# Attention layer: the last group's units in another order, and the last output tile's right half held in PSUM

## The chip, the cores and the metric

The kernel runs on one core of one Trainium2 chip. The metric is the device time of one execution in microseconds. TensorE (PE in the rows; its weight loads are PEld), VectorE (DVE), ScalarE (ACT) and GpSimd (POOL) each work through a queue of their own in order; SyncE (SP) issues most of the DMAs. Engines wait for one another by semaphores.

## The reference, cut to what matters

One layer: an RMS norm, an attention mixer with three branches, an output projection, a second RMS norm and the residual. S = 512 tokens, D = 1024, 16 heads of 64 in 4 groups of 4 heads (a group shares its keys and values).

```python
def rms_norm(x, gain):
    y = xf * lax.rsqrt(jnp.mean(xf * xf, axis=-1, keepdims=True) + RMS_EPS)
    return (y * gain.astype(jnp.float32)).astype(x.dtype)

def nsa_mixer(h, w_in, w_out, ...):
    q, kv, g, z = split_cols(h @ w_in, ...)
    gates, zs = jax.nn.sigmoid(g), jax.nn.silu(z)
    o_cmp, p_cmp = nsa_compressed(q, kc, vc, table)     # 31 compressed keys
    o_slc = nsa_selected(q, k_s, v_s, sel, table)       # with 8 blocks, all that are causal
    o_win = nsa_window(q, k_w, v_w, table)              # window of 512
    y = jnp.sum(gates * stack([o_cmp, o_slc, o_win]) * zs, axis=2)
    return y @ w_out                                     # (512 x 1024) @ (1024 x 1024)

h = x + rms_norm(nsa_mixer(rms_norm(x, pre_gain), ...), post_gain)
```

## The kernel before

Every float32 factor of a matmul is split into a high and a low part, and a product is three matmuls (high by high, high by low, low by high). `split_raw` makes the parts of a weight tile of 128x1024: a cast on ACT (L106, 1.05 us) and a subtraction on POOL (L109, 2.4 us); the raw tiles come by DMA into three buffers `wr`, the parts lie in three buffers each, `wh` and `wl`.

The attention goes over four groups g. A group has seven units: `win` for query tiles 3, 2, 1, then `both` (window and selected branch of query tile 0, and the compressed branch of all tiles), then `slc` for query tiles 1, 2, 3. A unit of query tile qt has qt + 1 key tiles. `qk(u)` makes its scores head by head (matmuls L582 into a bank `s`), DVE adds the bias and takes the extreme (L594), ACT exponentiates (L595). `pv(u)` transposes the probabilities (L676 into a bank `t`), ACT casts the high part `pth` (L679), DVE subtracts for the low part `ptl` (L680), and L684 and L685 multiply with the values into the one bank `o`. ACT copies the halves that are crossed (L690, L691), DVE adds them (L692, L693), POOL multiplies with the gate `zf` and adds into the group's `y` (L697, L698). In the last group `split_y(3, qt)` then casts the tile's y to a high part on ACT (L764), subtracts on DVE (L765), and puts qt on the list `ready`. `cmp_pv` is the compressed branch: two rounds of L747 to L749 in bank `o`, a product (L751) and an addition into y (L752) on DVE.

The program is written by hand in this order: `qk` of unit i is woven with `pv` of unit i - 1, and between their steps a generator `fill` is pulled for projections, at a rate per group; what is left of it at the end runs alone. The last piece of `fill` is `wout`, the output projection. For the halves c of the output columns it first accumulates the three finished groups (kp = 0, 1, 2; matmuls L804 to L806) in two banks `pj`, two tiles of rows at a time, and ACT copies the sums to `og` (L809). Then, for each tile t in the order of `ready` (0, 1, 2, 3), it adds the last group: per half six matmuls (L845 to L847) in a bank `pj`, an addition into `og` on DVE (L849), ACT's Square with its sum (L851); then the sum of both halves on POOL (L855), `rstd` on POOL (L85, L86), the gain multiplies (L853, L858 on POOL, L859 on DVE or POOL), and, one tile later, `finish`: `og * rstd + x` on DVE (L828) and the store (L829). PSUM has eight banks: two `pj`, three `s`, two `t`, one `o`.

The framework that builds the program gives each engine its instructions in an order of its own choosing near the written one; what that order is stands in the section on the change.

## Time and profile before

| | before |
|---|---|
| three timed runs | 486.06 us median, 485.45 to 486.08 |
| profiled execution | 485.76 us, of which the span of its instructions is 484.0 us |
| PE busy | 456.1 us (94%), mean granted clock 0.986 |
| DVE busy | 329.9 us (68%) |
| ACT busy | 274.2 us (57%) |
| POOL busy | 184.3 us (38%) |

The span goes from the first to the last instruction. Busy shares are means over stages with different limits. Matmuls are pipelined and their ends are modelled, so that one of 512 columns shows 0.39 us and the next starts 0.23 us after it.

### The profile page before, as it was taken

The page shows a single profiled execution, that of the slowest core. Times are in us where ns is not written, and L with a number is a line of the kernel's source. Part 1 is how long each engine was busy: PE and PEld are TensorE (multiplying, and loading weights), DVE is VectorE, ACT ScalarE, POOL GpSimd, SP SyncE. Part 2 cuts the span into 40 slices and gives each one's busy share as a digit, 9 for nine tenths or more (in the row PEclk, how much of TensorE's full clock was granted, in tenths as well). Part 3 has the DMA queues.
Part 4 walks back from the last instruction along what each step waited for, and adds up shares of the span by engine and source line. Part 5 has one row for each costly group of instructions (what it writes and reads, how often), then busy time and mean ns, then how long its engine had stood idle before and what let it go on. Part 6 is the DMA issues. An engine that isn't in the chain of part 4 may idle for free.

```text
span 484.0 us, 6882 instructions
## 1 busy us (share of the span) xinstructions
PE 456.1 (94%) x2330; PEld 375.2 (78%) x2330; DVE 329.9 (68%) x785; ACT 274.2 (57%) x644; POOL 184.3 (38%) x147
## 2 busy tenths in 40 slices
PE   5999999999999989999999999998899999999982
PEld 3898788878888768878888788886678888777761
DVE  6779752745456897665788874679867465876576
ACT  5613232436556858556587764576766456755541
POOL 3414543424124345333154343342514314342556
PEclk9989999999999999999999999999999999999996
DMA  8498455443023122321130511322152112031123
GB/s 289 140 90 256 141 165 173 126 137 80 16 82 86 41 70 65 112 85 45 43 110 1 175 44 45 87 53 58 45 173 86 46 45 87 1 89 43 57 75 130
DMA packets 45501, 44.63 MB, mean 92 GB/s; under 512 B 7751, under 2 KB 38471, under 8 KB 45466
## 3 DMA queue, kind: packets, MB, share of 16 engines
q1 hardware_dynamic: 44424, 44.00, 32.4%
q8 instruction: 18, 0.29, 0.3%
q10 hardware_dynamic: 1042, 0.20, 0.2%
q14 instruction: 17, 0.14, 0.1%
HBM read 41.99 MB, written 2.20 MB: 91 GB/s over the span
## 4 chain that ended last, share of the span: by engine, by line
PE 74%; ACT 9%; DVE 8%; POOL 4%; issue 3%; DMA 1%; POOLq 0%; SPq 0%; DVEq 0%; ACTq 0%
PE ps_pj L139 9%; PE ps_pj L137 9%; PE ps_pj L138 9%; PE ps_s L582 7%; PE ps_t L676 6%; PE ps_o L685 3%; ACT p L595 3%; PE ps_o L684 3%; PE ps_s L238 2%; PE ps_s L240 2%; PE ps_s L239 2%; PE ps_pj L239 2%; PE ps_pj L238 2%; PE ps_pj L240 2%; PE ps_s L667 1%
## 5 line engine op out<-in xcount | busy, mean ns | idle before, releaser
L109 POOL TENSOR_TENSOR wl<-wr,wh 128x1024 fp32r<-128x1024 f32 x49 | 118.5, 2419 | 163.7 <-ACT wh L106 150.2
L137 PE MATMUL ps_pj<-uh,wh 128*128 128x512 f32 x240 | 99.4, 414 | 0.0
L138 PE MATMUL ps_pj<-uh,wl 128*128 128x512 f32 x240 | 94.4, 393 | 0.0
L139 PE MATMUL ps_pj<-ul,wh 128*128 128x512 f32 x240 | 94.3, 393 | 0.0
L595 ACT ACTIVATE p<-p,nm 128x512 f32<-128x512 f32 (+3 forms) x128 | 71.6, 561 | 37.5 <-DVE nm L594 36.8
L106 ACT CAST wh<-wr 128x1024 fp32r<-128x1024 f32 x49 | 51.3, 1048 | 42.5 <-DMA wr<-in_nsa_w_in_dram 14.8
L680 DVE TENSOR_TENSOR ptl<-ps_t,pth 128x512 fp32r<-128x512 f32 x80 | 54.7, 686 | 21.0 <-ACT pth L679 20.5
L582 PE MATMUL ps_s<-kd,q 128*128 128x512 f32 (+5 forms) x256 | 61.7, 328 | 0.0
L679 ACT CAST pth<-ps_t 128x512 fp32r<-128x512 f32 x80 | 46.0, 579 | 23.1 <-PE ps_t L676 22.3
L139 PEld LDWEIGHTS ps_pj<-ul,wh 128*128 128x128 f32 x240 | 45.1, 188 | 9.9
L582 PEld LDWEIGHTS ps_s<-kd,q 128*128 128x128 f32 x256 | 45.4, 188 | 9.2 <-DVE nm L594 0.2
L594 DVE CUSTOM_DVE_ANT_0 p<-ps_s,bias 128x128 f32<-128x128 f32 (+3 forms) x80 | 34.7, 447 | 23.1 <-PE ps_s L582 22.6
L138 PEld LDWEIGHTS ps_pj<-uh,wl 128*128 128x128 f32 x240 | 45.3, 189 | 5.8
L137 PEld LDWEIGHTS ps_pj<-uh,wh 128*128 128x128 f32 x240 | 45.2, 188 | 5.3
L676 PE MATMUL ps_t<-ident,p 128*128 128x128 f32 x320 | 48.9, 272 | 0.0
L676 PEld LDWEIGHTS ps_t<-ident,p 128*128 128x128 f32 x320 | 39.3, 140 | 6.7
L684 PE MATMUL ps_o<-pth,vt 128*128 128x512 f32 x80 | 32.8, 411 | 2.5 <-DVE otmp L693 1.1
L685 PE MATMUL ps_o<-ptl,vt 128*128 128x512 f32 x80 | 32.5, 406 | 1.0 <-DVE ptl L680 1.0
L697 POOL TENSOR_TENSOR otmp<-otmp,zs 128x256 f32<-128x256 f32 x16 | 12.0, 748 | 48.4 <-DVE otmp L693 48.4
L695 POOL TENSOR_TENSOR y<-otmp,zs 128x256 f32<-128x256 f32 x16 | 11.8, 738 | 48.1 <-DVE otmp L693 48.1
L692 DVE TENSOR_TENSOR otmp<-ps_o,otmp 64x256 f32<-64x256 f32 x32 | 13.3, 415 | 21.8 <-ACT otmp L691 21.2
L594 DVE CUSTOM_DVE_ANT_1 p<-ps_s,bias 128x256 f32<-128x256 f32 (+2 forms) x48 | 25.9, 549 | 2.4 <-PE ps_s L582 2.1
(248 smaller groups left out, 899.8 us busy)
## 6 DMA issues: line engine op xcount, KB each, us to landing
wr<-in_nsa_w_in_dram SPq DMA_DIRECT2D x36, 512.0 KB, 3.7
wr<-in_nsa_w_in_dram SPq DMA_DIRECT2D x16, 256.0 KB, 4.3
bias<-toepd SPq DMA_DIRECT2D x16, 256.0 KB, 6.8
wr<-in_nsa_w_out_dram SPq DMA_DIRECT2D x8, 512.0 KB, 4.3
xt<-in_x_dram SPq DMA_DIRECT2D x4, 512.0 KB, 4.2
wr<-in_nsa_cmp_k_w_dram SPq DMA_DIRECT2D x4, 512.0 KB, 5.3
wr<-in_nsa_cmp_v_w_dram SPq DMA_DIRECT2D x4, 512.0 KB, 3.7
xr<-in_x_dram SPq DMA_DIRECT2D x8, 256.0 KB, 2.8
```

What stands on the lines that cost most here:

```text
L106: A.copy(h[:, 0:kn], raw[:, 0:kn])
L109: el.tensor_tensor(l[:, 0:kn], raw[:, 0:kn], h[:, 0:kn].bitcast(F32), op=ALU.subtract)
L137: T.matmul(p, a, rh, start=k == 0, stop=False)
L138: T.matmul(p, b, rh, start=False, stop=False)
L139: T.matmul(p, a, rl, start=False, stop=k == KT - 1)
L582: T.matmul(po, qs[h][:, qt * 128:(qt + 1) * 128], kds[h // R][:, i, c0:c0 + n], start=i == 0, stop=i == 1)
L594: V.tensor_tensor_reduce(pd, src, bi, 1.0, BIG, ALU.add, ALU.min, st["nm"][:, hh:hh + 1])
L595: A.activation(po, po, AF.Exp, bias=st["nm"][:, hh:hh + 1], scale=-1.0, accum_out=st["rs"][:, hh:hh + 1])
L676: T.transpose(tp[:, hh * 128:(hh + 1) * 128], st["p"][hh][:, c:c + 128], ident)
L680: V.tensor_tensor(pl, tp, ph.bitcast(F32), op=ALU.subtract)
L684: T.matmul(acc, v, prev[1], start=j == 1, stop=False)
L685: T.matmul(acc, v, prev[2], start=False, stop=j == qt + 1)
```

## The change

In the last group the three `slc` units run in the order 3, 2, 1, and `wout` takes its tiles in the order 0, 3, 2, 1 (`turn`); the compressed branch's gate is projected ahead of the selected one's in that group. The right half (c = 1) of the last tile is left out of the early accumulation. Its three finished groups are accumulated ahead of the third tile's last-group matmuls (18 matmuls, moved) into a bank `late`, the last group's six matmuls go into the same bank, and Square and the gain multiply read that bank, with no copy to `og` and no addition. The last group's weights `w3` get buffers of their own, those of earlier tiles. For the last two tiles the last group's sums use the banks `s`. The mean's 1/1024 goes into the Square as a scale of 1/32, and `rstd` adds both halves' sums and EPS in one instruction (L88 after; the power is L90). For the last unit the gate product and the addition into y, and for the last two tiles three gain multiplies, go from POOL to DVE. Line numbers after the change are higher: L582 is L589, L594 and L595 are L601 and L602, L667 is L674, L676 to L693 are L683 to L700, L695, L697 and L698 are L703, L705 and L706, L742 is L750, L764 and L765 are L772 and L773, L106 is L113, L804 to L806 stay and serve the last group too, L809 is L819, L828 is L841, L849 is L862, L851 is L864, L858 is L870, L859 is L871 (L866 for the last tile).

```diff
-    def rstd(dst, ss):
-        tc.keep_in_program_order(P.tensor_scalar(dst, ss, 1.0 / D, EPS, op0=ALU.mult, op1=ALU.add))
+    def rstd(dst, ss, other=None):
+        if other is None:
+            i = P.tensor_scalar(dst, ss, EPS, None, op0=ALU.add)
+        else:
+            i = P.tensor_scalar(dst, ss, other, EPS, op0=ALU.add, op1=ALU.add)
+        tc.keep_in_program_order(i)
         tc.keep_in_program_order(P.tensor_tensor(dst, dst, nhalf, op=ALU.pow))
...
-             (("win", 3), ("win", 2), ("win", 1), ("both", 0), ("slc", 1), ("slc", 2), ("slc", 3))]
+             [("win", 3), ("win", 2), ("win", 1), ("both", 0)] + [("slc", (t, 4 - t)[g == 3]) for t in (1, 2, 3)]]
...
+            eng = V if u == units[-1] else P
             if br == B_WIN:
-                P.tensor_tensor(y[:, :, qsl], tmp, zf, op=ALU.mult)
+                eng.tensor_tensor(y[:, :, qsl], tmp, zf, op=ALU.mult)
             else:
-                P.tensor_tensor(tmp, tmp, zf, op=ALU.mult)
-                P.tensor_tensor(y[:, :, qsl], y[:, :, qsl], tmp, op=ALU.add)
+                eng.tensor_tensor(tmp, tmp, zf, op=ALU.mult)
+                eng.tensor_tensor(y[:, :, qsl], y[:, :, qsl], tmp, op=ALU.add)
...
     def wout():
+        turn = [0, 3, 2, 1]
         og = [keep.tile([128, D], F32, name="og", tag="u", bufs=8) for _ in range(NT)]
         sumsq = const.tile([128, NT, 2], F32, name="sumsq")
 
-        def wo_tile(kp, c):
+        def wo_tile(kp, c, home=None):
             raw = load_raw([((lambda raw: raw.rearrange("p (k a) c -> p k (a c)", k=2)),
                              w_out[kp * 256:(kp + 1) * 256, c * S:(c + 1) * S].rearrange("(k p) c -> p k c", p=128))])
-            return [v.rearrange("p (k a) c -> p k (a c)", k=2) for v in split_raw(raw, 4, A, P)]
+            return [v.rearrange("p (k a) c -> p k (a c)", k=2) for v in split_raw(raw, 4, A, P, home)]
+
+        def wo_mm(p, kp, t, a, b, first, last):
+            ts = slice(t * 128, (t + 1) * 128)
+            for kk in range(2):
+                yh, yl = yhl[kp][0][:, kk, ts], yhl[kp][1][:, kk, ts]
+                T.matmul(p, yh, a[:, kk], start=first and kk == 0, stop=False)
+                T.matmul(p, yl, a[:, kk], start=False, stop=False)
+                T.matmul(p, yh, b[:, kk], start=False, stop=last and kk == 1)
+                yield 650
 
         for c in range(2):
             cs = slice(c * S, (c + 1) * S)
             w = [wo_tile(kp, c) for kp in range(3)]
             yield 0
-            for tp in range(2):
-                ps_ = [pj(), pj()]
+            for pair in (turn[0:2], turn[2:4 - c]):
+                ps_ = [pj() for _ in pair]
                 for kp in range(3):
-                    for t in range(2):
-                        ts = slice((tp * 2 + t) * 128, (tp * 2 + t + 1) * 128)
-                        for kk in range(2):
-                            k = kp * 2 + kk
-                            yh, yl = yhl[kp][0][:, kk, ts], yhl[kp][1][:, kk, ts]
-                            a, b = w[kp][0][:, kk], w[kp][1][:, kk]
-                            T.matmul(ps_[t], yh, a, start=k == 0, stop=False)
-                            T.matmul(ps_[t], yl, a, start=False, stop=False)
-                            T.matmul(ps_[t], yh, b, start=False, stop=k == 5)
-                            yield 650
-                for t in range(2):
-                    A.copy(og[tp * 2 + t][:, cs], ps_[t])
-        w = [wo_tile(3, c) for c in range(2)]
+                    for p, t in zip(ps_, pair):
+                        yield from wo_mm(p, kp, t, *w[kp], kp == 0, kp == 2)
+                for p, t in zip(ps_, pair):
+                    A.copy(og[t][:, cs], p)
+        while (3, B_CMP) not in zdone:
+            yield None
+        w3 = [wo_tile(3, 0, [keep.tile([128, 4, 256], F32R, name="w3", tag="u", bufs=8) for _ in range(2)]),
+              wo_tile(3, 1, [at.tile([128, 4, 256], F32R, name="w3", tag="zs", bufs=3) for _ in range(2)])]
...
         prev = None
-        for j in range(NT):
+        for j, t in enumerate(turn):
+            if j == 2:
+                late = pj()
+                for kp in range(3):
+                    yield from wo_mm(late, kp, turn[3], *w[kp], kp == 0, False)
             while len(ready) <= j:
                 yield None
-            t = ready[j]
+            assert ready[j] == t
             for i in range(2):
                 SP.dma_start(xrs[j][i], x[t * 128:(t + 1) * 128, i * S:(i + 1) * S])
             os_ = [og[t][:, i * S:(i + 1) * S] for i in range(2)]
             for i in range(2):
-                p = pj()
-                ts = slice(t * 128, (t + 1) * 128)
-                for kk in range(2):
-                    yh, yl = yhl[3][0][:, kk, ts], yhl[3][1][:, kk, ts]
-                    a, b = w[i][0][:, kk], w[i][1][:, kk]
-                    T.matmul(p, yh, a, start=kk == 0, stop=False)
-                    T.matmul(p, yl, a, start=False, stop=False)
-                    T.matmul(p, yh, b, start=False, stop=kk == 1)
-                    yield 650
-                V.tensor_tensor(os_[i], os_[i], p, op=ALU.add)
+                held = j == 3 and i == 1
+                p = late if held else sb() if j >= 2 else pj()
+                yield from wo_mm(p, 3, t, *w3[i], not held, True)
+                src = p if held else os_[i]
+                if not held:
+                    V.tensor_tensor(os_[i], os_[i], p, op=ALU.add)
                 junk = at.tile([128, S], F32, name="junk", tag="lc", bufs=1)
-                A.activation(junk, os_[i], AF.Square, accum_out=sumsq[:, t, i:i + 1])
-                if i == 0 and j == 3:
-                    P.tensor_tensor(os_[0], os_[0], gb[0], op=ALU.mult)
+                A.activation(junk, src, AF.Square, scale=1.0 / 32, accum_out=sumsq[:, t, i:i + 1])
+                if j == 3:
+                    V.tensor_tensor(os_[i], src, gb[i], op=ALU.mult)
             ss = const.tile([128, 1], F32, name="fss", tag="fss", bufs=4)
-            P.tensor_tensor(ss, sumsq[:, t, 0:1], sumsq[:, t, 1:2], op=ALU.add)
-            rstd(ss, ss)
+            rstd(ss, sumsq[:, t, 0:1], sumsq[:, t, 1:2])
             if j < 3:
                 P.tensor_tensor(os_[0], os_[0], gb[0], op=ALU.mult)
-            (P if j == 2 else V).tensor_tensor(os_[1], os_[1], gb[1], op=ALU.mult)
+                V.tensor_tensor(os_[1], os_[1], gb[1], op=ALU.mult)
             if prev is not None:
                 finish(*prev)
             prev = t, xrs[j], ss
...
-        fills += [zproj(g, B_SLC), zproj(g, B_CMP)]
+        fills += [zproj(g, b) for b in ((B_SLC, B_CMP), (B_CMP, B_SLC))[g == 3]]
```

The three places that follow are those on which the working rests.

**ACT, from the cast of the compressed branch's transposes (`cph`) in the last group.** `og` is a copy out of a bank `pj`, `y_4558` and `y_4564` are the high part of the last group's y, `p,rs` the exponents of the next unit's scores, `wh` weights for c = 1, `w_4805` and `w_4811` those of `w3`. Before:

```order
L742 CAST cph<-ps_t 128x512
L690 COPY otmp<-ps_o 64x256
L691 COPY otmp<-ps_o 64x256
L106 CAST wh<-wr 128x1024
L679 CAST pth<-ps_t 128x512
L595 ACTIVATE p,rs<-p,nm 128x384
L764 CAST y_4558<-y 128x2x128
L809 COPY og<-ps_pj 128x512
L679 CAST pth<-ps_t 128x512
L595 ACTIVATE p,rs<-p,nm 128x384
L809 COPY og<-ps_pj 128x512
L106 CAST wh<-wr 128x1024
```

After:

```order
L750 CAST cph<-ps_t 128x512
L113 CAST wh<-wr 128x1024
L772 CAST y_4564<-y 128x2x128
L113 CAST wh<-wr 128x1024
L602 ACTIVATE p,rs<-p,nm 128x384
L686 CAST pth<-ps_t 128x512
L819 COPY og<-ps_pj 128x512 x2
L602 ACTIVATE p,rs<-p,nm 128x384
L686 CAST pth<-ps_t 128x512
L602 ACTIVATE p,rs<-p,nm 128x384 x2
L113 CAST w_4805<-wr 128x1024
L113 CAST w_4811<-wr 128x1024
```

The y cast and the third weight cast now stand ahead of the next unit's first exponent and first `pth`, and both copies of `og` behind that `pth`; the casts of `w3` follow at the end of this piece, where before they stood among the last unit's `pth` casts.

**TensorE, the same place: from the first scores of the next unit** (128x384, the unit of query tile 2). Before:

```order
L582 MATMUL ps_s<-kd,q 128x384 x2
L667 MATMUL ps_s<-ident,f_4499 128x128 x2
L676 MATMUL ps_t<-ident,p 128x128 x4
L804 MATMUL ps_pj<-wh,yhl 128x512
L805 MATMUL ps_pj<-wh,yhl 128x512
L806 MATMUL ps_pj<-wl,yhl 128x512
L582 MATMUL ps_s<-kd,q 128x384 x2
L804 MATMUL ps_pj<-wh,yhl 128x512
L805 MATMUL ps_pj<-wh,yhl 128x512
L806 MATMUL ps_pj<-wl,yhl 128x512
L676 MATMUL ps_t<-ident,p 128x128 x4
L804 MATMUL ps_pj<-wh,yhl 128x512
```

After:

```order
L589 MATMUL ps_s<-kd,q 128x384 x2
L804 MATMUL ps_pj<-wh,yhl 128x512
L805 MATMUL ps_pj<-wh,yhl 128x512
L806 MATMUL ps_pj<-wl,yhl 128x512
L674 MATMUL ps_s<-ident,f_4505 128x128 x2
L683 MATMUL ps_t<-ident,p 128x128 x4
L589 MATMUL ps_s<-kd,q 128x384 x2
L683 MATMUL ps_t<-ident,p 128x128 x4
L589 MATMUL ps_s<-kd,q 128x384 x4
L691 MATMUL ps_o<-pth,vt 128x512
L589 MATMUL ps_s<-kd,q 128x256
L804 MATMUL ps_pj<-wh,yhl 128x512
```

The matmuls of the output projection (L804 to L806) that stood between the scores and transposes are behind them now: two transposes, all four heads' scores, the first product with the values and half of the next unit's first score (128x256) come first.

**DVE, the last instructions.** `og<-og,ps` is the addition of the last group's sums, `og,pgain` the gain multiply, `xr` the last step of an output half. Before:

```order
L859 TENSOR_TENSOR og<-og,pgain 128x512
L828 SCALAR_TENSOR_TENSOR xr<-og,fss,xr 128x512
L849 TENSOR_TENSOR og<-og,ps_pj 128x512
L828 SCALAR_TENSOR_TENSOR xr<-og,fss,xr 128x512
L849 TENSOR_TENSOR og<-og,ps_pj 128x512
L859 TENSOR_TENSOR og<-og,pgain 128x512
L849 TENSOR_TENSOR og<-og,ps_pj 128x512
L828 SCALAR_TENSOR_TENSOR xr<-og,fss,xr 128x512 x2
L849 TENSOR_TENSOR og<-og,ps_pj 128x512 x2
L828 SCALAR_TENSOR_TENSOR xr<-og,fss,xr 128x512 x2
L859 TENSOR_TENSOR og<-og,pgain 128x512
L828 SCALAR_TENSOR_TENSOR xr<-og,fss,xr 128x512 x2
```

After:

```order
L705 TENSOR_TENSOR otmp<-otmp,zs 128x256
L841 SCALAR_TENSOR_TENSOR xr<-og,fss,xr 128x512
L706 TENSOR_TENSOR y<-y,otmp 128x2x128
L871 TENSOR_TENSOR og<-og,pgain 128x512
L773 TENSOR_TENSOR y_4565<-y,y_4564 128x2x128
L841 SCALAR_TENSOR_TENSOR xr<-og,fss,xr 128x512 x3
L862 TENSOR_TENSOR og<-og,ps_s 128x512 x3
L871 TENSOR_TENSOR og<-og,pgain 128x512
L841 SCALAR_TENSOR_TENSOR xr<-og,fss,xr 128x512
L866 TENSOR_TENSOR og<-og,pgain 128x512
L866 TENSOR_TENSOR og<-ps_pj,pgain 128x512
L841 SCALAR_TENSOR_TENSOR xr<-og,fss,xr 128x512 x3
```

The products with the gate (`otmp<-otmp,zs`, `y<-y,otmp`) are among them now, the additions read banks `s`, the held half has a multiply from `ps_pj` in place of an addition, and three steps `xr` stand at the end where there were two.

## Rows read from the trace of the kernel before

**Rows 1.** The span, and busy time by stretch near the end. Columns: stretch in us, its length, then busy us (and number of instructions) of PE, PEld, DVE, ACT and POOL, then the granted TensorE clock as a share of full speed, the DMA share and GB/s.

```profile
span 484.0 us, 6882 instructions
...
456.00:466.00 10.00, 9.93 (x46) 7.85 (x45) 4.63 (x8) 4.97 (x12) 5.69 (x6) 1.00 0.28 95
...
466.00:476.00 10.00, 7.27 (x24) 5.18 (x22) 8.58 (x10) 2.92 (x9) 7.54 (x11) 0.83 0.28 106
...
476.00:484.00 8.00, 0.00 (x0) 0.00 (x0) 4.42 (x5) 0.70 (x2) 3.46 (x5) 0.59 0.35 131
```

**Rows 2.** Timeline of the end: start in us, duration in us, engine, line, operation, output and inputs, shapes, and in brackets the idle time before it with what ended it.

```profile
459.01 0.39 PE L685 MATMUL ps_o<-ptl,vt 128*128 128x512 f32 x1
...
460.22 0.42 DVE L692 TENSOR_TENSOR otmp<-ps_o,otmp 64x256 f32<-64x256 f32 x1 [1.79 <-ACT otmp L691]
...
466.88 0.39 PE L847 MATMUL ps_pj<-wl,y 128*128 128x512 f32 x1
...
469.16 0.50 PE L845 MATMUL ps_pj<-wh,y 128*128 128x512 f32 x1 [1.89 <-DVE og L849]
...
471.12 0.63 PE L846 MATMUL ps_pj<-wh,y 128*128 128x512 f32 x1
...
474.77 0.39 PE L847 MATMUL ps_pj<-wl,y 128*128 128x512 f32 x1
```

**Rows 3.** Waits of TensorE's weight loads from 411 to 484 us: who waited for whom, us in total, times, longest.

```profile
PEld ps_pj L845 <- DVE og L849: 2.8, 2, 2.3
...
PEld ps_o L685 <- DVE ptl L680: 1.4, 2, 0.8
...
PEld ps_pj L804 <- ACT og L809: 0.7, 1, 0.7
...
PEld ps_s L667 <- issue: 0.7, 1, 0.7
```

**Rows 4.** Timeline of the last steps, columns as in rows 2.

```profile
475.19 0.69 DVE L849 TENSOR_TENSOR og<-og,ps_pj 128x512 f32<-128x512 f32 x1 [0.48 <-PE ps_pj L847]
...
475.36 0.19 POOL L85 TENSOR_SCALAR fss<-fss 128x1 f32<-128x1 f32 x1
...
475.63 0.55 POOL L86 TENSOR_TENSOR fss<-fss,nhalf 128x1 f32<-128x1 f32 x1
...
475.97 0.63 ACT L851 ACTIVATE junk<-og 128x512 f32<-128x512 f32 x1 [0.44 <-DVE og L849]
...
476.15 1.26 POOL L853 TENSOR_TENSOR og<-og,pgain 128x512 f32<-128x512 f32 x1
...
477.37 0.64 POOL L855 TENSOR_TENSOR fss<-sumsq 128x1 f32<-128x1 f32 x1
...
478.10 0.57 POOL L85 TENSOR_SCALAR fss<-fss 128x1 f32<-128x1 f32 x1
...
478.75 0.88 POOL L86 TENSOR_TENSOR fss<-fss,nhalf 128x1 f32<-128x1 f32 x1
...
479.66 1.42 DVE L828 SCALAR_TENSOR_TENSOR xr<-og,fss,xr 128x512 f32<-128x512 f32 x2 [0.44 <-POOL fss L86]
```

**Rows 5.** Timeline, DVE and POOL side by side at two places.

```profile
425.70 2.38 POOL L109 TENSOR_TENSOR wl<-wr,wh 128x1024 fp32r<-128x1024 f32 x1
...
425.81 2.82 DVE L752 TENSOR_TENSOR y<-y,ctmp 128x512 f32<-128x512 f32 x1
...
429.63 0.68 DVE L752 TENSOR_TENSOR y<-y,ctmp 128x512 f32<-128x512 f32 x1
...
466.68 1.27 POOL L858 TENSOR_TENSOR og<-og,pgain 128x512 f32<-128x512 f32 x1
...
466.75 1.75 DVE L828 SCALAR_TENSOR_TENSOR xr<-og,fss,xr 128x512 f32<-128x512 f32 x1 [1.00 <-POOL fss L86]
```

**Rows 6.** Timeline, ACT and TensorE at 430 us.

```profile
430.40 0.41 ACT L764 CAST y<-y 128x256 fp32r<-128x256 f32 x1
...
430.71 0.58 ACT L809 COPY og<-ps_pj 128x512 f32<-128x512 f32 x1
...
431.19 0.59 ACT L679 CAST pth<-ps_t 128x512 fp32r<-128x512 f32 x1
...
431.34 0.50 PE L804 MATMUL ps_pj<-wh,yhl 128*128 128x512 f32 x1 [0.40 <-ACT og L809]
```

**Rows 7.** Groups of instructions from 412 to 484 us, by line and shape: count, busy us in total, mean ns of one, idle us before them and what ended it.

```profile
L849 DVE TENSOR_TENSOR og<-og,ps_pj 128x512 f32<-128x512 f32 x8 | 5.5, 682 | 0.9 <-PE ps_pj L847 0.9
...
L859 DVE TENSOR_TENSOR og<-og,pgain 128x512 f32<-128x512 f32 x3 | 2.0, 683 | 0.1
...
L595 ACT ACTIVATE p<-p,nm 128x384 f32<-128x384 f32 x4 | 2.4, 614 | 1.7 <-DVE nm L594 1.7
...
L106 ACT CAST wh<-wr 128x1024 fp32r<-128x1024 f32 x5 | 5.2, 1047 | 1.5 <-PE ps_pj L805 1.5
...
L668 DVE TENSOR_TENSOR zs<-zs,ps_s 128x256 f32<-128x256 f32 x5 | 2.1, 411 | 0.0
```

**Rows 8.** Timeline of TensorE at 326 us, and the stretch around it (columns as in rows 1).

```profile
326.41 0.40 PE L139 MATMUL ps_pj<-ul,wh 128*128 128x512 f32 x1
...
328.38 0.41 PE L667 MATMUL ps_s<-ident,f 128*128 128x128 f32 x2 [1.57 <-DVE f L639]
...
324.00:328.00 4.00, 2.80 (x16) 2.07 (x14) 4.00 (x8) 3.06 (x9) 2.38 (x1) 1.00 0.50 155
```

More of the change, by code (lines that the diff above doesn't have):

```diff
@@ L100, in load_raw, with split_raw @@
         return raw
-    def split_raw(raw, kn, eh, el):
-        h = wp.tile([128, 4, 256], F32R, name="wh", tag="wh", bufs=3)
-        l = wp.tile([128, 4, 256], F32R, name="wl", tag="wl", bufs=3)
+    def split_raw(raw, kn, eh, el, home=None):
+        if home is not None:
+            h, l = home
+        else:
+            h = wp.tile([128, 4, 256], F32R, name="wh", tag="wh", bufs=3)
+            l = wp.tile([128, 4, 256], F32R, name="wl", tag="wl", bufs=3)
         if eh is A:
@@ L296, in rms @@
             ss = a1.tile([128, 1], F32, name="ss", bufs=4)
-            tc.keep_in_program_order(A.activation(sq, xs[t], AF.Square, accum_out=ss))
+            tc.keep_in_program_order(A.activation(sq, xs[t], AF.Square, scale=1.0 / 32, accum_out=ss))
             r = a1.tile([128, 1], F32, name="r", bufs=4)
```

## Prediction

> **What bounds the kernel now.** I read the table of ten-microsecond stretches first. From 456 to 466 us TensorE is busy 9.93 of 10, and the earlier attention groups look the same; from 466 to 476 it is busy only 7.27 while DVE and POOL are at 8.58 and 7.54, and from 476 on it does nothing [rows 1]. So the kernel is bound by TensorE nearly to the end, and the end has two parts of its own: a stretch in which TensorE waits, and a tail without TensorE.
>
> The first part is in the timeline of TensorE. The last attention matmul starts at 459.01, so the next could start at 459.24; 51 matmuls of 512 columns are left. The 33rd behind it starts at 466.88 [rows 2]: 7.87/33 = 0.238 us each with a wait of 0.5 in it (2.8 less 2.3, [rows 3]), 0.223 without; I take 0.23. At that pace the last would start at 459.24 + 50 x 0.23 = 470.7. It starts at 474.77. The 4.1 us between are a wait for DVE's add that frees one of the two `pj` banks (matmul at 469.16; the list of waits gives L845 2.8 us in two waits, [rows 3]) and a stretch after it in which the granted clock is at the lower of its two levels, 1.2 GHz, and a matmul takes 0.63 instead of 0.39 us [rows 2]; the clock's mean over 466 to 476 is 0.83 [rows 1].
>
> The second part runs from that matmul's end, 474.77 + 0.39 = 475.16, to the span's end, 484.0: 8.84 us. The reader is to see in [rows 4] that it is a chain of small steps: DVE's add (ends 475.88), ACT's Square with its read-out (to about 476.70), POOL's sum of two columns, which starts only after POOL's gain multiply (476.15 to 477.41), POOL's scale-and-EPS, POOL's power (ends 479.63), two DVE steps (end 481.08), and 2.9 us for the stores.
>
> **The change, part by part.** The sum is made against the profiled execution, 485.76 us with a span of 484.0, so 1.76 us lie outside; the median of the three timed runs is 486.06, 0.3 above it.
>
> *Four banks instead of two, and the held half.* The number of matmuls stays; after the last attention matmul there are still 51. The held half costs no banks that the tail lacks: the tiles of the last two rounds now come from the three `s` banks, which attention no longer uses. TensorE next waits for DVE's add in two places, before the right half of the second tile and before the held sums, and both have 0.9 us or more of matmuls in between, against an add of 0.68 [rows 7]. I therefore take back the whole 4.1 us, clock included: the clock fell behind the idle time, and that is gone. Last matmul: starts at 470.7, ends at 471.1. From below: a wait of 0.5 could remain at each of the two places, 1.0 in all. From above the pace of 0.223 would give 4.4.
>
> *The falling order in the last group.* The last attention unit is now two key tiles instead of four, but that buys nothing by itself: TensorE reaches the last output tile 39 matmuls, 9.0 us, after the last attention matmul, and the unit's way from there through ACT, DVE and its cast takes about 4 us. It does cost something earlier. The big unit's softmax now runs beside the short `both` unit, and on ACT the program has the cast of the first y tile, the third weight cast, an exponent, and only then the cast `pth` that TensorE waits for, and behind it the two copies that free the `pj` banks. The y cast needs DVE's two y adds; in the trace the first is held by POOL and takes 2.82 us, the second 0.68, and the y cast ran at 430.40 [rows 5, 6]. The same POOL instruction stands in the same place now, so I put the y cast at 430.25 to 430.66 again. Then 1.05 (weight cast), 0.61 (exponent), 0.59 (`pth`) and 0.48 (first copy, the step from 430.71 to 431.19) follow [rows 6, 7]: `pth` at 432.85, the first bank free at 433.35, against 431.77 and 431.28 before. TensorE's score of the fourth head waits about 0.5 for a bank `s` (till 431.5), the product behind it 1.0 for `pth`, and the first matmul of c = 1 about 0.5 for its bank `pj`: 2.0 us. Near the end two waits of 0.15 and 0.5 for the last unit's `pth` and `ptl` come in, since a two-tile unit leaves less between its steps. New waits: 2.65. The old order's waits go: 1.4, 0.7 and 0.7 us, 2.8 in all [rows 3]. The difference is nothing, with 2 us to either side: more if ACT is later, less if the scores run ahead.
>
> *Fewer steps at the end.* The held half has no copy by ACT and no add by DVE: 0.78 (475.19 to the Square's start at 475.97) goes from the path. POOL's sum and EPS become one instruction, which saves 0.73 (477.37 to 478.10), and POOL's gain multiply goes to DVE, which saves the wait of 0.67 (476.70 to 477.37) [rows 4]. One POOL step is 0.19 us when nothing holds it and 0.57 here; the power is 0.55 and 0.88 [rows 4]. The changed program makes DVE's gain multiply of the held half wait for the Square that reads the same bank, so DVE's steps behind the last matmul are: Square 0.09 + 0.73, multiply 0.77, the second tile-2 step 0.71, and two steps of 0.71. With 2.9 for the store that is 6.65 us behind the last matmul's end instead of 8.84; the POOL steps (0.2 + 0.1 + 0.55) lie beside the multiply. TensorE's chain would end at 471.1 + 6.65 = 477.8.
>
> *DVE's own queue.* With TensorE earlier, DVE is next: it takes over work from POOL. It starts the last unit's two otmp adds at 460.22 now [rows 2]; then one Square (0.63 and its read-out) stands between ACT's two copies ahead of them, so 460.9. From there its list is 2 adds of 0.42, 4 adds from PSUM of 0.68, 3 steps of 0.42 (the product, its sum into y, the low part of y), 4 gain multiplies of 0.68 and 8 last steps of 0.71 (1.42 for two [rows 4]; others by [rows 7]): 0.84 + 2.72 + 1.26 + 2.72 + 5.68 = 13.2. To it come waits for POOL. A DVE step that reads two SBUF tensors while POOL multiplies takes 1.75 instead of 0.71 [rows 5], so 1.0 each; POOL still has three gain multiplies, of which the first lies beside DVE steps from PSUM. From below 0, from above 3.0; by where they stand in the program I take half a wait for each of the two others, 1.0. And DVE waits about 1.0 for the norm factor of the third tile (POOL 0.19 + 0.55 and the hand-overs). 460.9 + 13.2 + 2.0 = 476.1, and 2.9 for the store: 479.0. This is later than TensorE's chain by 1.2 us, so it sets the end.
>
> The Trainium skill, "SBUF — State Buffer", section "Who interferes with whom", speaks against moving work to DVE: it says that a DVE instruction with two SBUF inputs and a GpSimd instruction that reads SBUF exclude each other, the later one blocked until the first is done. The trace agrees: 425.81 + 2.82 ends 0.55 after POOL's 425.70 + 2.38 [rows 5]. By that rule alone, with every one of the three multiplies met at its start, DVE's end would be 2.0 later than I take, a span of 481.0 and no more gain than 3.0.
>
> *At nothing:* the mean's factor inside the Square, since the instruction stays one; the weights' new homes, since their casts keep their number (ACT has 2.1 us of them before two `pth` casts; TensorE has some 5 us of other matmuls there, and if that cover is gone they cost up to 2.1); the swapped projections of the last group, since the order on TensorE up to 411.8 is the same.
>
> Sum: 484.0 - 479.0 = 5.0 us less; 485.76 - 5.0 = 480.8 against the profile, 481.1 beside the timed runs.
>
> **The rivals.**
> *ACT's queue at 431 to 434 us costs more.* For it speaks that TensorE's next work there hangs on ACT in program order alone. If the wait is 2.4 longer (the y cast later by one held add, 2.1, and a hand-over), the last matmul ends at 473.5 and the span at 480.2: 482.2 us. If the clock falls after it too, as it did at about 470 (8 matmuls lost 0.19 each, 1.5), 483.7. Against the clock: a gap of 1.57 us at 326.4 to 328.4 left it at 1.00 [rows 8].
> *DVE is not held.* Waits of 0 instead of 1.0: its list ends at 475.1, the span at 478.0: 480.1 us, or 479.6 if TensorE keeps the faster pace and DVE's wait for the norm factor shrinks with it. For it: most of DVE's steps at that time read PSUM.
> *The change doesn't do what it says.* The bank waits go, but DVE gives it back: three waits of 1.0, and DVE starts 2 later with the last unit; 483.0 to 484, 485 to 486 us. Against it: DVE's list is 13.2 us long where it had 20.9.
> *Slower.* Place: ACT's y cast. It must be late enough that TensorE's last matmul comes 6.2 us later than I take (5.0 and the 1.2 of slack). I find 2.1 for a second held add, 1.5 for the clock and 2.1 for the weight casts ahead of two `pth`: 5.7. So all three must happen and a little more; then 486.5 to 488.
>
> **How the numbers follow.** What a measurement of this kernel can tell from no change is about 0.2%, 1 us. The forecast case, 480.2 to 482.2 us, gets 0.57; ACT's longer queue 0.22; DVE not held 0.09; no gain 0.07; slower 0.05. The first three are faster: 0.88. The range from 479.6 to 484.6 leaves out the last two cases and a little at the lower end.
>
> **What would show it.** After 459 us no wait of a matmul on DVE's add above 0.5 and no lower clock before the last matmul; that matmul ending at 470 to 472.5; a wait for `pth` and for `og`'s copy of 1 to 2 us together at 431 to 434; 6 to 7 us from the last matmul to the end, DVE busy throughout. The prediction is wrong if TensorE idles several us at 430 to 436, if the clock falls there, or if DVE's last steps start after 477.

## The result and the profile after

The changed kernel takes 481.0 us (478.9 to 482.2) beside 486.07 us for the kernel before; its ratio to before is 0.9885, 95% interval 0.984 to 0.993. Timed once more among the experiments it took 480.66 us, ratio 0.9877 (0.985 to 0.9903). So it is faster by 5 to 6 us; the forecast was 481.1.

The profiled execution took 481.59 us. By stretch (columns as in [rows 1]):

```profile
span 479.8 us, 6876 instructions
...
416.00:426.00 10.00, 9.47 (x46) 7.22 (x44) 8.03 (x21) 8.28 (x18) 4.92 (x4) 1.00 0.01 2
426.00:436.00 10.00, 8.63 (x42) 6.60 (x43) 8.61 (x17) 4.12 (x9) 5.97 (x4) 1.00 0.31 107
...
456.00:466.00 10.00, 9.78 (x47) 7.56 (x46) 8.53 (x17) 5.14 (x15) 5.92 (x7) 1.00 0.00 0
466.00:476.00 10.00, 6.52 (x29) 5.07 (x27) 8.42 (x14) 3.17 (x9) 4.72 (x6) 0.97 0.35 132
476.00:480.00 4.00, 0.00 (x0) 0.00 (x0) 0.88 (x2) 0.00 (x0) 0.00 (x0) 0.50 0.52 197
```

The reader is to see that the granted clock stays at 1.00 until TensorE is done at 472.5 (the 0.97 at 466 to 476 takes in idle time behind that; it was 0.83 in [rows 1]), and that TensorE now loses time at 426 to 436. Its waits from 411 us on (columns as in [rows 3]):

```profile
PEld ps_o L692 <- DVE ptl L687: 1.7, 5, 0.5
PEld ps_o L755 <- issue: 1.5, 1, 1.5
PEld ps_o L691 <- ACT pth L686: 0.9, 1, 0.9
PEld ps_s L589 <- DVE zs L675: 0.5, 1, 0.5
PEld ps_o L755 <- DVE ctmp L759: 0.3, 1, 0.3
PEld ps_pj L804 <- ACT og L819: 0.2, 1, 0.2
```

The wait for DVE's add, 2.8 us in [rows 3], is gone. The last steps, to be held against [rows 4]:

```profile
472.13 0.39 PE L806 MATMUL ps_pj<-w,y 128*128 128x512 f32 x1
...
472.74 0.60 ACT L864 ACTIVATE junk<-ps_pj 128x512 f32<-128x512 f32 x1
472.94 0.75 DVE L841 SCALAR_TENSOR_TENSOR xr<-og,fss,xr 128x512 f32<-128x512 f32 x1 [0.45 <-POOL fss L90]
...
473.61 0.68 DVE L866 TENSOR_TENSOR og<-og,pgain 128x512 f32<-128x512 f32 x1
...
474.21 0.69 DVE L866 TENSOR_TENSOR og<-ps_pj,pgain 128x512 f32<-128x512 f32 x1
474.46 0.56 POOL L90 TENSOR_TENSOR fss<-fss,nhalf 128x1 f32<-128x1 f32 x1
474.81 2.07 DVE L841 SCALAR_TENSOR_TENSOR xr<-og,fss,xr 128x512 f32<-128x512 f32 x3
```

From the last matmul's end (472.52) to the span's end it is 7.28 us, where it was 8.84.

**A finer measure.** Executions of one kernel differ by up to 5 us, and the profiles show about 4 us of spread ahead of the place that the change touches (the mark's times in the table below). A mark helps: the last projection matmul (`ps_pj<-ul,wh`). In every kernel the same 328 matmuls follow it (236 of 512 columns, 68 of 128, and 8 each of 256, 288 and 384), only in another order. The time from its start to the span's end I call the rest. In the profile of before it starts at 401.53, so the rest is 484.0 - 401.53 = 82.47 us; here it is 77.05:

```profile
402.75 0.40 PE L146 MATMUL ps_pj<-ul,wh 128*128 128x512 f32 x1
```

and in the second run of the changed kernel 479.4 - 402.29 = 77.11. The two agree to 0.06 us, while their spans differ by 0.4. The gain in the part that the change touches is 5.4 us. The experiments are compared by the rest too; one of them, late_cast, has none, because its profiled execution was a disturbed one. Every rest is read from one profile, and the two of the changed kernel are the only repetition.

### The profile page after: what moved, and what is told of

Same layout as the page of the kernel before. It is cut to its first block, busy times and chain, and to the rows that moved or that the text cites. A ratio compares the mean times of both kernels' runs of the same rounds, so it can differ in the third digit from the quotient of the medians.

```text
span 479.8 us, 6876 instructions
## 1 busy us (share of the span) xinstructions
PE 455.1 (95%) x2330; PEld 375.7 (78%) x2330; DVE 325.8 (68%) x788; ACT 273.6 (57%) x643; POOL 178.7 (37%) x139
## 4 chain that ended last, share of the span: by engine, by line
PE 79%; DVE 8%; ACT 7%; issue 2%; DMA 1%; POOL 1%; SPq 0%; DVEq 0%; ACTq 0%
PE ps_pj L146 9%; PE ps_pj L144 9%; PE ps_pj L145 9%; PE ps_s L589 7%; PE ps_t L683 6%; PE ps_o L692 4%; PE ps_o L691 3%; ACT p L602 2%; PE ps_pj L804 2%; PE ps_s L245 2%; PE ps_pj L806 2%; PE ps_pj L805 2%; PE ps_s L246 2%; PE ps_s L247 2%; PE ps_pj L246 2%
## 5 line engine op out<-in xcount | busy, mean ns | idle before, releaser
L116 POOL TENSOR_TENSOR wl<-wr,wh 128x1024 fp32r<-128x1024 f32 x47 | 113.7, 2418 | 160.7 <-ACT wh L113 146.0
L602 ACT ACTIVATE p<-p,nm 128x512 f32<-128x512 f32 (+3 forms) x128 | 71.7, 561 | 35.5 <-DVE nm L601 34.9
L113 ACT CAST wh<-wr 128x1024 fp32r<-128x1024 f32 x47 | 49.2, 1047 | 40.9 <-DMA wr<-in_nsa_w_in_dram 14.7
L687 DVE TENSOR_TENSOR ptl<-ps_t,pth 128x512 fp32r<-128x512 f32 x80 | 54.7, 686 | 22.5 <-ACT pth L686 21.9
L589 PE MATMUL ps_s<-kd,q 128*128 128x512 f32 (+5 forms) x256 | 62.2, 330 | 0.2 <-DVE zs L675 0.2
L589 PEld LDWEIGHTS ps_s<-kd,q 128*128 128x128 f32 x256 | 45.2, 188 | 9.3 <-DVE zs L675 0.5
L601 DVE CUSTOM_DVE_ANT_0 p<-ps_s,bias 128x128 f32<-128x128 f32 (+3 forms) x80 | 34.7, 447 | 23.1 <-PE ps_s L589 22.6
L683 PE MATMUL ps_t<-ident,p 128*128 128x128 f32 x320 | 48.7, 272 | 0.0
L683 PEld LDWEIGHTS ps_t<-ident,p 128*128 128x128 f32 x320 | 39.1, 140 | 6.3
L703 POOL TENSOR_TENSOR y<-otmp,zs 128x256 f32<-128x256 f32 x16 | 11.8, 737 | 47.1 <-DVE otmp L700 47.0
L705 POOL TENSOR_TENSOR otmp<-otmp,zs 128x256 f32<-128x256 f32 x15 | 11.2, 748 | 45.9 <-DVE otmp L700 45.9
L699 DVE TENSOR_TENSOR otmp<-ps_o,otmp 64x256 f32<-64x256 f32 x32 | 13.2, 414 | 21.8 <-ACT otmp L698 21.3
L601 DVE CUSTOM_DVE_ANT_1 p<-ps_s,bias 128x256 f32<-128x256 f32 (+2 forms) x48 | 26.0, 550 | 2.1 <-PE ps_s L589 1.8
```

What stands on the lines that cost most here:

```text
L113: A.copy(h[:, 0:kn], raw[:, 0:kn])
L116: el.tensor_tensor(l[:, 0:kn], raw[:, 0:kn], h[:, 0:kn].bitcast(F32), op=ALU.subtract)
L589: T.matmul(po, qs[h][:, qt * 128:(qt + 1) * 128], kds[h // R][:, i, c0:c0 + n], start=i == 0, stop=i == 1)
L601: V.tensor_tensor_reduce(pd, src, bi, 1.0, BIG, ALU.add, ALU.min, st["nm"][:, hh:hh + 1])
L602: A.activation(po, po, AF.Exp, bias=st["nm"][:, hh:hh + 1], scale=-1.0, accum_out=st["rs"][:, hh:hh + 1])
L683: T.transpose(tp[:, hh * 128:(hh + 1) * 128], st["p"][hh][:, c:c + 128], ident)
```

## The experiments

The kernel before was timed again beside every group of runs (medians 486.2 to 486.8 us); the ratios are to these times, so medians of different rows are compared less well than ratios or rests.

| kernel | median us | ratio to before (95%) | mark at | rest us | last matmul's end to span's end |
|---|---|---|---|---|---|
| before | 486.07 | 1 | 401.53 | 82.47 | 8.84 |
| changed, run again (after_again) | 480.66 | 0.9877 (0.985-0.9903) | 402.29 | 77.11 | 7.3 |
| order_only | 488.89 | 1.0067 (1.0043-1.0091) | 400.82 | 85.08 | 8.8 |
| old_order | 484.43 | 0.9952 (0.993-0.9975) | 402.28 | 79.92 | 7.8 |
| two_banks | 484.99 | 0.9966 (0.9948-0.9984) | 402.41 | 81.19 | 9.5 |
| no_hold | 484.62 | 0.9963 (0.9937-0.9988) | 401.64 | 81.16 | 10.9 |
| hold_pj | 480.76 | 0.9886 (0.9848-0.9924) | 401.84 | 77.16 | 7.3 |
| no_hold_less | 485.28 | 0.9977 (0.9956-0.9997) | 399.98 | 82.02 | 12.0 |
| after_less | 481.94 | 0.9891 (0.9864-0.9918) | 403.07 | 77.13 | 7.3 |
| hold_two | 482.3 | 0.9899 (0.9865-0.9933) | 403.56 | 77.24 | 7.0 |
| low_on_dve | 479.46 | 0.9847 (0.9814-0.9879) | 404.17 | 75.63 | 7.3 |
| late_cast | 479.86 | 0.9856 (0.9822-0.989) | - | - | - |
| best | 477.59 | 0.9811 (0.9786-0.9836) | 401.82 | 73.88 | 6.7 |

**after_again**: no edit.

> The changed kernel once more, as the yardstick of the runs beside it: 481.0 again, 480.3 to 482 (ratio 0.987 to 0.991).

It came as expected.

**order_only**: the falling order put into the kernel before.

```
-  ("slc", 1), ("slc", 2), ("slc", 3)
+  ("slc", (t, 4 - t)[g == 3]) for t in (1, 2, 3)
```

> The kernel before with the falling order alone. Theory: no gain, 485 to 488; TensorE's wait for the add that frees a bank (2.8 us) and the stretch at 1.2 GHz are still there behind the last attention matmul. Rival (the order buys the end): 481 to 483.

Slower by 0.67%, a little beyond the theory's range and far from the rival's; the rest is 2.6 us longer. The waits for the bank and the lower clock behind them (0.83 at 468 to 478) are still there, with new waits beside them:

```profile
PEld ps_pj L845 <- DVE og L849: 3.1, 2, 2.3
PEld ps_o L685 <- DVE ptl L680: 2.4, 4, 1.6
PEld ps_pj L845 <- ACT og L809: 1.6, 2, 1.4
PEld ps_o L747 <- issue: 1.5, 1, 1.5
```

**old_order**: the changed kernel with rising order.

```
-  ("slc", (t, 4 - t)[g == 3])          turn = [0, 3, 2, 1]
+  ("slc", t)                           turn = [0, 1, 2, 3]
```

> Undoes one part: the last group's units run in rising size again (slc 1, 2, 3; output tiles 0, 1, 2, 3); the held half, the extra banks and the shorter end stay. Theory (the gain is made behind the last attention matmul, the order is neutral within 2 us): 481 us, 479 to 483, and the waits of the old order at 412 to 456 (2.8 us in all) are back while the wait for the late y cast at 432 is gone. Rival (the small last unit is what buys the end): 484 to 486.

The rival's number, 484.4, though order_only has refuted it as a rule: the rest is 79.92, so inside the whole change the falling order is worth 2.8 us. The theory's old waits are back, but the order isn't neutral. TensorE's waits behind the mark add up to 7.6 us where the changed kernel has 5.1. The largest:

```profile
PEld ps_o L691 <- ACT pth L686: 2.1, 2, 1.7
PEld ps_pj L804 <- ACT og L819: 1.7, 2, 1.0
PEld ps_pj L804 <- DVE og L862: 1.2, 1, 1.2
```

Of these, 2.7 us lie at 447 to 451 and 1.2 at 465. The same order costs 2.6 us alone and gives 2.8 us with the other parts: it can't be priced by itself.

**no_hold** and **two_banks**: the last tile's right half is summed during the attention as the others are; two_banks has the two `pj` banks alone besides.

```
no_hold:    - late = pj(); its 18 matmuls at j == 2      + held = False; turn[2:4] for both c
two_banks:  also  - p = sb() if j >= 2 else pj()         + p = pj()
```

> The changed kernel without the held half: the last tile's right half is summed over groups 0 to 2 during the attention, copied out and added by DVE as the others are; the extra banks, the order and the shorter end stay. Theory (the held half only takes DVE's add, 0.78 us, from the path): 481.8 to 482.5. Rival (its 18 matmuls are the cover for the last unit's steps, and without them TensorE waits 2 us or more for the last y casts and the clock falls): 484 to 486.

> As no_hold, and the last two tiles use the two pj banks again, as before the change. Theory (the two banks cost the 4.1 us of waits and lower clock behind the last attention matmul): 485 to 486.5, with matmuls that wait for DVE's add 2 us or more and a granted clock below 0.9 before the last matmul. Rival (DVE's queue sets the end whatever the banks): as no_hold within 0.7.

no_hold has the rival's number without its reason (TensorE's waits behind the mark are 6.0 us where they were 5.1, and the granted clock is 1.00 until its last matmul): without the held half the rest is 4.1 us longer, not 0.8. two_banks, by its time, lies at the lower edge of the theory's range and in its rival's, but the two kernels are the same to 0.03 us of the rest (81.16, 81.19), and that is its rival's answer: the banks are worth nothing. two_banks does have the wait that I had charged to the banks, and with it a later end of the last matmul (71.7 us behind the mark where no_hold has 70.3):

```profile
PEld ps_pj L804 <- DVE og L858: 2.3, 2, 1.9
```

but the clock did not fall behind it before the last matmul (1.00 at 466 to 476), and what TensorE lost was hidden: TensorE's work was not what the end waited for. In no_hold its work ended 10.9 us before the span did:

```profile
462.40 0.69 DVE L858 TENSOR_TENSOR og<-og,ps_pj 128x512 f32<-128x512 f32 x1
...
471.54 0.39 PE L806 MATMUL ps_s<-w,y 128*128 128x512 f32 x1
...
478.49 1.41 DVE L841 SCALAR_TENSOR_TENSOR xr<-og,fss,xr 128x512 f32<-128x512 f32 x2 [0.45 <-POOL fss L90]
```

The first row is DVE's first add of the tail, 60.8 us behind the mark. In the changed kernel it comes 54.7 us behind it:

```profile
457.40 0.68 DVE L862 TENSOR_TENSOR og<-og,ps_pj 128x512 f32<-128x512 f32 x1
```

So the held half brings the first output tile forward by 6.1 us: its 18 matmuls no longer stand ahead of that tile on TensorE, but behind the last attention unit.

**hold_pj**: the held half in one `s` bank, all other halves in the two `pj` banks.

```
-  late = pj()      p = late if held else sb() if j >= 2 else pj()
+  late = sb()      p = late if held else pj()
```

> The changed kernel with the held half kept (in one s bank), but with the two pj banks alone for all other halves of the tail. Theory formed from no_hold and two_banks (the banks buy nothing, since DVE's queue ends last; the held half buys by putting 18 matmuls between the last attention unit and the last two tiles, so that DVE finishes the first two tiles beside them): as the changed kernel within 1 us, 480.5 to 482. Rival (the prediction's step: two banks cost up to 4.1 us of waits and lower clock): 483 to 485.

The theory's number: 77.16. The extra banks are worth nothing with the held half either, and here for another reason: no matmul waits for DVE's add at all (TensorE's waits behind the mark are the changed kernel's, one by one), and the last matmul ends 69.8 us behind the mark in both.

**no_hold_less** and **after_less**: two of DVE's gain multiplies left out (1.4 us).

```
-  V.tensor_tensor(os_[1], os_[1], gb[1], op=ALU.mult)
+  if j == 2: V.tensor_tensor(os_[1], os_[1], gb[1], op=ALU.mult)
```

> no_hold with two DVE steps left out: the gain multiply of the right half of the first two output tiles (that part of the output stays without its gain). Theory (without the held half DVE's queue sets the end): the end comes earlier by the two steps, 1.4 us, and up to 2.4 if a step held by POOL goes with them: 482.2 to 483.2 where no_hold had 484.6. Rival (TensorE's matmuls or their banks set it): 484.3 to 485.

> The same two DVE steps left out of the changed kernel (the right half of two output tiles stays without its gain). Theory (with the held half DVE has caught up before the last matmul, so its list length there no longer counts): as the changed kernel, 480.3 to 481. Rival (DVE's list of 13.2 us sets the end of the changed kernel too, as the prediction had it): 1.4 us earlier, 479.3 or less.

after_less came as the theory had it: the rest stays (77.13), so the length of DVE's list does not set the end of the changed kernel. no_hold_less refutes the theory: the rest grew by 0.9 us. Its rival's number is near, but TensorE was done 12.0 us before the end. So neither TensorE sets the end there, nor the length of DVE's list alone. Its timeline shows what does:

```profile
464.04 0.57 POOL L90 TENSOR_TENSOR fss<-fss,nhalf 128x1 f32<-128x1 f32 x1
...
464.64 2.45 DVE L841 SCALAR_TENSOR_TENSOR xr<-og,fss,xr 128x512 f32<-128x512 f32 x2 [0.77 <-POOL fss L90]
...
467.01 0.67 DVE L858 TENSOR_TENSOR og<-og,ps_pj 128x512 f32<-128x512 f32 x1
...
468.99 0.57 POOL L90 TENSOR_TENSOR fss<-fss,nhalf 128x1 f32<-128x1 f32 x1
...
469.52 1.27 POOL L866 TENSOR_TENSOR og<-og,pgain 128x512 f32<-128x512 f32 x1
469.59 1.75 DVE L841 SCALAR_TENSOR_TENSOR xr<-og,fss,xr 128x512 f32<-128x512 f32 x1 [1.31 <-POOL fss L90]
471.26 0.67 DVE L858 TENSOR_TENSOR og<-og,ps_s 128x512 f32<-128x512 f32 x1
```

DVE's program has the last step of a tile (`xr`) ahead of an add for the next tile. That step waits for POOL's norm factor; the add then feeds ACT's Square, and that feeds POOL's next factor. It is a ring DVE, ACT, POOL, DVE, with one tile a turn: the factors end at 464.6, 469.6, 474.2 and 477.7 here, at 466.6, 471.2, 474.1 and 478.5 in no_hold, and at 466.7, 471.7, 476.2 and 479.6 in the kernel before. A turn takes 3 to 5 us, and the end comes 4.3 to 4.4 us behind the last factor in all three, so in these kernels the end is set by when the first factor is ready and by how long the turns take. The first factor ends 64.6, 64.9 and 65.2 us behind the mark in no_hold_less, no_hold and the kernel before, and the three turns take 13.0, 11.9 and 12.9: no_hold_less starts 0.3 earlier and turns 1.1 slower, which is its 0.9. About 1 us of a turn is a DVE step beside POOL's gain multiply: the `xr` at 469.59 takes 1.75 us beside POOL's 469.52 to 470.79, as one did before [rows 5], where three take 2.07 in the changed kernel's tail. That the ring is the cause is read from the traces; no run breaks it by itself, and none separates the earlier start from these held steps. That a shorter list made the turns slower may come from the scheduler, which then placed DVE's steps otherwise; this stays open.

**hold_two**: both last tiles' right halves held.

```
-  late = pj(), 18 matmuls for turn[3]        held = j == 3 and i == 1
+  lates = [pj(), pj()], 36 for turn[2:4]     held = j >= 2 and i == 1
```

> The changed kernel with the right halves of the last two tiles held in the two pj banks, so 36 matmuls instead of 18 stand between the last attention unit and the last two tiles. Theory (more room for DVE is worth nothing once DVE has caught up; the 18 matmuls are missing beside the attention, where TensorE then waits more): 480.5 to 483. Rival (each held half buys what the first one did, 3 to 4 us): 477 to 478.

As the theory had it (77.24). With one held half the end already follows TensorE's last matmul, 7.3 us behind it; the second brings DVE's first add forward by another 2.7 us (51.9 behind the mark) and buys nothing.

**low_on_dve**: the second column block's low halves on DVE.

```
-  split_raw(raw, 4, A, P, home)
+  split_raw(raw, 4, A, V if c and home is None else P, home)
```

> The changed kernel with the low halves of the second column block's weights (three subtractions of 1024 columns) on DVE instead of POOL. Theory (POOL's subtractions hold the DVE steps with two SBUF inputs at 424 and 429, and the wait of 1.5 us before the first cph product and the y cast at 432.4 come from that): the wait goes, the y cast is back near 430.5, 479 to 480. Rival (three more steps of about 1.1 us in DVE's own queue take their place): 481 to 483.

The rest is 1.45 us shorter; by the timed runs alone the interval overlaps that of the changed kernel. In the changed kernel POOL's subtractions stand beside two DVE steps:

```profile
422.96 2.39 POOL L116 TENSOR_TENSOR wl<-wr,wh 128x1024 fp32r<-128x1024 f32 x1 [1.15 <-PE ps_o L691]
...
424.31 1.32 DVE L648 TENSOR_TENSOR f<-f,gate 128x256 f32<-128x256 f32 x1
...
426.52 0.19 PEld L755 LDWEIGHTS ps_o<-cph,vb 128*128 128x128 f32 x1 [1.50 <-issue]
...
428.06 2.40 POOL L116 TENSOR_TENSOR wl<-wr,wh 128x1024 fp32r<-128x1024 f32 x1
...
428.78 2.23 DVE L760 TENSOR_TENSOR y<-y,ctmp 128x512 f32<-128x512 f32 x1
...
432.43 0.41 ACT L772 CAST y<-y 128x256 fp32r<-128x256 f32 x1 [5.88 <-DVE y L760]
```

With the subtractions moved, the first of the two takes 0.43 us, and the wait of TensorE's weight loads ahead of L755 falls from 1.5 to 0.6 us (at the matmul itself from 1.09 to 0.23):

```profile
425.89 0.43 DVE L648 TENSOR_TENSOR f<-f,gate 128x256 f32<-128x256 f32 x1
...
427.35 0.47 PE L755 MATMUL ps_o<-cph,vb 128*128 128x512 f32 x1 [0.23 <-DVE otmp L700]
```

L755 needs the bank that DVE frees with L699 and L700, which stand behind L648. The y cast came only 0.4 us earlier (433.47, which is 29.3 us behind the mark, where it was 29.7) and not the 1.9 forecast, so this half of the theory failed. TensorE's waits behind the mark fall from 5.1 to 3.5 us, of which 1.2 lie ahead of L755. The last matmul ends 1.4 us earlier behind the mark and the tail stays 7.3: in the changed kernel the end follows TensorE, so here a wait on TensorE has its full price.

**late_cast**: the first y cast emitted behind the next unit's second `pth` cast.

```
-  split_y(g, 0) in pv of "both" for g == 3
+  if u == units[25] and j == 1: split_y(3, 0), behind pth and ptl
```

> The changed kernel with the first y cast of the last group emitted behind the next unit's second pth cast. Theory (pth and the copies of og stand behind the late y cast on ACT): the waits for pth and og at 434 to 435, 1.1 us, shrink to under 0.3: 480. Rival (TensorE waits there for DVE's work, not for ACT's order): as the changed kernel within 0.5.

479.86 is the theory's number, but the interval of the ratio overlaps that of the changed kernel, and without its profile the waits can't be read; by itself it is unclear.

**best**: both edits above, and gain multiplies of the last two tiles that don't write in place.

```
+  gs = [at.tile([128, S], F32, name="gm", tag="p", bufs=8) for _ in range(2)] if j >= 2 else os_
-  op(os_[i], ..., gb[i], mult)
+  op(gs[i], ..., gb[i], mult)
```

> The changed kernel with three edits: low_on_dve, late_cast, and the gain multiplies of the last two tiles write into tiles of their own, so that they need not wait for the Square that reads the same half. Theory (the first two each take 1.2 us from TensorE's waits at 424 to 436, in part the same ones; the third lets POOL's factor of the third tile come 0.5 earlier and takes DVE's wait of 0.45 from the tail): 478 to 479. Rival (the two edits mend the same wait, and DVE's wait in the tail is followed by another): 479.3 to 480.

477.59 us, ratio 0.9811: faster than both kernels. The rest is 3.2 us shorter than the changed kernel's, more than the theory had. Of TensorE's 5.1 us of waits behind the mark 2.2 are left, in two groups:

```profile
PEld ps_o L694 <- DVE ptl L687: 1.6, 5, 0.5
PEld ps_o L755 <- ACT cph L750: 0.6, 1, 0.6
```

and the tail is 6.7 us instead of 7.3. What late_cast and the third edit give each isn't separated.

## Why the prediction was right, and where its reasons were not

The total was right (5.0 us forecast, 5.4 behind the mark), but its terms were not: errors of 3 to 4 us cancelled, and that they did was luck. Measured by the rest, one part after the other: the falling order 82.47 to 85.08; then the shorter end, the weights' homes, the gate products on DVE and the swapped gate projections together 85.08 to 81.19 (no run takes them apart; 3.0 of these 3.9 us are there already at POOL's first factor, which ends 67.9 us behind the mark in order_only and 64.9 in two_banks); the banks nothing; the held half 81.16 to 77.1. The shorter end moves two gain multiplies from POOL to DVE, not the three that the section on the change names.

- *Four banks, 4.1 us.* **Wrong.** What I read in [rows 2, 3] was there, a wait and a slower clock on TensorE, and both went, but without the held half TensorE was not what the end waited for, and with it the wait is gone on two banks as well (hold_pj). The rows of the tail already hinted at it: POOL's two factors there end at 476.2 and 479.6 [rows 4], a whole turn of the ring, of which I read only the steps of the last tile.
- *Held half, 0.78 us.* **Wrong by a factor of five**: 4.1 us. I counted the add it removes and took the 18 matmuls it moves as neutral since TensorE's sum stays. They moved the first tile forward by 6.1 us, and with that the end no longer waits for the ring.
- *Falling order, new waits 2.65.* The five waits were right in sum: 0.5, 1.0, 0.5, 0.15 and 0.5 forecast, 0.51, 0.94, 0.19, 0.41 and 0.54 measured, 2.59; singly the third and fourth are off by 0.3. Missed was the wait of 1.5 at 426.5 (0.2 before). And the net of nothing, with 2 us to either side, holds for neither surrounding: +2.6 alone, -2.8 with the rest.
- *y cast at 430.25 to 430.66.* Measured 432.43 to 432.84; of this 1.2 us is the later mark, so it came 1.0 late.
- *Last matmul's end at 471.1.* Measured 472.52, less 1.2 for the mark 471.3. Right, with no clock fall and no wait on DVE's add before it, as forecast; but hold_pj, without the banks, has the same.
- *6.65 us from there.* 7.28: DVE waits 0.45 for POOL's factor of the third tile, and the left half's multiply stands in the chain, which I had left out.
- *DVE's own queue sets the end, 476.1.* The time was near (476.88), the reason **wrong**: after_less shortens that list by 1.4 us and the end stays. DVE still waits at 472.94 for POOL's factor of the third tile, so what it had to do before that doesn't count; in the kernels with the held half and the falling order the end comes 6.7 to 7.3 us behind the last matmul, wherever that lies. And the 20.9 that I held against the list's 13.2 was DVE's time from 460.22 to 481.08 with its waits, not the length of its list.
- *DVE steps held by POOL, 1.0 in the tail.* In the changed kernel's tail almost none: the three steps at 466.73 take 2.06 together, 0.69 each (in no_hold_less one takes 1.75). The rule of the Trainium skill, "SBUF — State Buffer", section "Who interferes with whom", was weighed in the wrong place. The trace agrees with it at 424 and 428 us, where 0.42 became 1.32 and a y add took 2.23, as one had taken 2.82 before [rows 5]; TensorE lost 1.3 us more there than before.
- *The weights' homes at nothing.* Not tried alone, so open.

## What to carry to other kernels

When several steps of one tile pass through three engines, look at when the first tile's chain starts before counting the steps of the last one: moving 18 matmuls from ahead of it gave 4.1 us, and two more banks gave nothing. A wait on the busiest engine is worth its length only if that engine's work is what the end waits for; the time between its last instruction and the end tells. Parts of a change are priced by undoing each in the whole change as well as by adding each alone, since the same order here cost 2.6 us alone and gave 2.8 with the rest.

## What was not expected of the hardware

The mark came at 399.98 to 404.17 us in the thirteen profiles, 4 us apart, although TensorE's 2002 matmuls up to it come in the same order in all of them; the 77 us behind it repeated to 0.06 us in the changed kernel. A part is the granted clock. The second profile of the changed kernel has it at 0.83 in one stretch of the common code:

```profile
20.00:30.00 10.00, 10.00 (x78) 9.36 (x77) 7.09 (x19) 2.88 (x6) 2.48 (x3) 1.00 0.83 85
...
350.00:360.00 10.00, 9.16 (x41) 7.52 (x42) 6.79 (x16) 5.02 (x12) 1.88 (x3) 0.83 0.59 182
```

(the clock is the third number from the end). In its first profile it was the other way round, 0.83 and 1.00; in low_on_dve, where the mark comes latest, both are 0.83, and in best both are 1.00. Over the thirteen profiles the mark comes at 399.98 to 401.82 where neither stretch is at 0.83 (four profiles), at 401.53 to 403.56 where one is (eight), and at 404.17 where both are. Why the clock differs, and the rest of the spread, are not explained. And removing two DVE steps made a kernel 0.9 us slower behind the mark (no_hold_less).
